# Retention with left-over keys: keys copied by VectorE, values rounded two steps earlier, values stored in rows of 4 KB

## The chip, the cores and the metric

The kernel runs on one core of a Trainium2 chip, in one launch. The metric is device time in microseconds, the median of several runs. TensorE (PE) multiplies, VectorE (DVE), ScalarE (ACT) and GpSimd (POOL) work on its results, SyncE (SP) and POOL issue nearly all DMAs, each on a queue of its own.

## What is computed

The reference is one block of a language model over 528 tokens, 16 meta tokens and 512 real ones: a gated feed-forward layer, a mixer, a second feed-forward layer and a norm. The change lies in the mixer's retention branch. It has four heads with keys of 256 and values of 512 elements. Cut to what matters:

```python
qm, km, vm = q[:, :, :N_META], k[:, :, :N_META], v[:, :, :N_META]          # N_META = 16
state0 = einsum('bhkd,bhke->bhde', km * zeta_m, vm)
def step(state, qkv):                                                      # chunks of 128 tokens
    inner = (qc @ kc.T * d_in) @ vc
    cross = (qc @ state) * xi
    state = g_chunk * state + (kc * zeta).T @ vc
    return state, inner + cross
y = y * rsqrt(mean(y * y) + EPS)
yr = (silu(rg) * y) @ w_ret_out
```

That is the same as causal scores times a decay, times the values. The kernel computes it in that form: for 512 queries and 528 keys, scores times a decay table, then scores times values.

## The kernel before

**Products.** Matmul operands are split in two float32r parts, a high part (ScalarE rounds, `AF.Copy`) and a low part (VectorE subtracts the high part); each product is three matmuls, high by high, high by low, low by high. `steps_through` runs a list of steps. A step has its weight tile loaded (SP), rounded by ScalarE (`upper`, two steps ahead) and its low part made by VectorE (`lower`, called inside an earlier step). TensorE, VectorE and ScalarE work in the order in which the program is written, through the retention part SP too. POOL's order is found by the scheduler that lays out the program: among what is ready, what was written first goes first.

**Values.** The class `Values` (L1333) makes values, gates and attention values of the real tokens two blocks of 128 at a time and stores them in DRAM (`leave`, L1370). `vrs_d` holds head, token, column. The values of the 16 meta tokens come from `last_tokens` (L1395) and are stored in `vd`.

**Where the tokens lie.** In the scores the 528 keys are the 16 meta tokens first. The four full blocks of 128 keys therefore end 16 tokens short of a block of real tokens, and the last 16 keys that a block of 128 queries can see are left over. They are "the last tokens": `last_of` (L1298) names them among the keys, `corner_keys` (L1839) copies them together, `corners` (L1846) multiplies them with the last 16 queries of each block, and one further matmul in `weigh` (L1875) adds their part of the output: its operands are `ptail` (the left-over scores: 32 rows high, 32 low, 32 high again, for two blocks at a time) and `vtail` (the left-over values: high, high again, low). `place_last` (L1624) loads the left-over values to three places of `vtail` by six DMAs on POOL's queue; `split_last` (L1631) rounds two of the three on ScalarE and returns the subtract that makes the third on VectorE.

**One head.** `fetch_head` (L1747) loads values and gates on SP's queue, the values by four DMAs: 112 rows, the meta tokens, and three more blocks. `values_in` (L1767) splits them. `decayed` (L1820) makes four blocks of scores (`psst`, 512 to 128 columns), multiplies each with the decay table (L1828, VectorE, into a buffer `tmp`), and splits it: ScalarE rounds a block, and VectorE makes its low part behind the next block's product. `weigh` (L1864) multiplies scores and values for one block of queries; ScalarE squares and sums the result, VectorE multiplies it with the gate.

**Order in time.** Head 0 is special. The gate steps `start_0` and `start_1` (L2079, L2090) load it, split its values and, in `after_1` (L2083), run `decayed(0)`, the low half of the values, the Silu of its gates and `index_keys(0)` on POOL. The next step, the first query projection of head 1, has 24 matmuls in eight groups of three, 0 to 7; ahead of groups 2 and 5 (L2116) stand `corner_keys` and `corners(0)`, and behind it `weigh_all(0)` (L2094). For heads 1 to 3 the four steps of `outputs(h)` (L1999), each two groups `j` of 12 matmuls, carry the next head: step 0 fetches it, step 1 ends with `values_in`, step 2 with `decayed`, step 3 begins with `corner_keys`, has `corners` behind its first group (after `lower` and `beside`, which does a step of the top-k search on VectorE) and ends with `weigh_all`. From head 1 on, POOL adds each group's output to `accr` (L2025) and makes the low parts of the values (L1774).

**Buffers.** `tmp()` gives one of four buffers of one tag; a buffer is free again when the last reader of its tile is done. `ka` and `kb_`, the index keys and their swapped copy, take two of the four before `decayed(0)` (loads at L1698 and L1700); `index_keys(0)` (L1729 to L1731, on POOL) is the last to read `kb_`, `index_keys(2)` the last to read `ka`. Blocks of scores and other results of up to 512 columns share four PSUM banks (`sm_tile`).

```python
            for kb in range(4):                                   # decayed, L1823
                t = tmp()[:, :n]
                TT(t, ps, u[0][:, :n], ALU.mult)
                low()                                             # low part of the block before
                low = in_two(t, ph, pl)                           # ScalarE now, VectorE later
```

## Time and profile before

| | us |
|---|---|
| median of 3 runs (1478.28 to 1480.94) | 1480.2 |
| the profiled execution's own time | 1479.45 |
| its span, first to last instruction | 1477.5 |
| PE busy | 1460.5 |
| DVE busy | 1153.3 |
| ACT busy | 785.8 |
| POOL busy | 292.4 |

The profile is one execution, taken by the hardware. The span is a little shorter than the execution's own time. A line such as L1875 is a line of the kernel; "out<-in" names the tiles that an instruction writes and reads, and a number in brackets is the time its engine stood idle before it, with what ended that. Of TensorE two rows exist, PE for matmuls and PEld for weight loads; matmuls overlap in the pipeline, so one of 512 columns shows about 0.39 us and the next begins earlier. PEclk is the clock granted to TensorE as a share of 2.4 GHz: 1.00, or 0.50 for 1.2 GHz. Times in timelines count from the start of the span. The mean granted clock of this execution is 0.996.

### The profile page before, as it was taken

The page shows a single profiled execution, that of the slowest core. Times are in us where ns is not written, and L with a number is a line of the kernel's source. Part 1 is how long each engine was busy: PE and PEld are TensorE (multiplying, and loading weights), DVE is VectorE, ACT ScalarE, POOL GpSimd, SP SyncE. Part 2 cuts the span into 40 slices and gives each one's busy share as a digit, 9 for nine tenths or more (in the row PEclk, how much of TensorE's full clock was granted, in tenths as well). Part 3 has the DMA queues.
Part 4 walks back from the last instruction along what each step waited for, and adds up shares of the span by engine and source line. Part 5 has one row for each costly group of instructions (what it writes and reads, how often), then busy time and mean ns, then how long its engine had stood idle before and what let it go on. Part 6 is the DMA issues. An engine that isn't in the chain of part 4 may idle for free.

```text
span 1477.5 us, 22534 instructions
## 1 busy us (share of the span) xinstructions
PE 1460.5 (99%) x8626; PEld 1288.5 (87%) x8626; DVE 1153.3 (78%) x1694; ACT 785.8 (53%) x1137; POOL 292.4 (20%) x363
## 2 busy tenths in 40 slices
PE   9999999999999999999999999999999999999998
PEld 8999999999988888788878788888888888888887
DVE  5998888876887887578778798888657787767776
ACT  6656455455354554467454547777534644434444
POOL 1101111102100001331152442444102221201110
PEclk9999999999999999999999999999999999999999
DMA  5458887556644543564437343767756576466323
GB/s 173 102 157 202 190 186 188 138 127 222 218 149 160 172 161 132 177 196 165 125 122 224 111 150 101 216 176 200 222 183 210 164 219 200 142 199 202 126 79 122
DMA packets 211516, 247.75 MB, mean 168 GB/s; under 512 B 32176, under 2 KB 154024, under 8 KB 211408
## 3 DMA queue, kind: packets, MB, share of 16 engines
q1 hardware_dynamic: 173168, 179.77, 38.4%
q0 software_dynamic: 34320, 59.70, 16.5%
q10 hardware_dynamic: 3920, 6.84, 1.4%
q8 instruction: 68, 1.11, 0.3%
q14 instruction: 40, 0.33, 0.1%
HBM read 206.73 MB, written 39.34 MB: 167 GB/s over the span
## 4 chain that ended last, share of the span: by engine, by line
PE 92%; DVE 3%; ACT 2%; DMA 2%; issue 1%; ACTq 0%; DVEq 0%; SPq 0%
PE psd L2851 8%; PE psqX L2684 7%; PE psvX L1444 7%; PE psqX L162 7%; PE psqZ L162 5%; PE psd L162 4%; PE psqY L2684 4%; PE psvY L1444 4%; PE psak L162 3%; PE psrk L162 3%; PE psaq L162 3%; PE psga L162 3%; PE psat L162 3%; PE psmo L162 3%; PE psrq L162 3%; PE psdX L162 2%
## 5 line engine op out<-in xcount | busy, mean ns | idle before, releaser
L330 DVE TENSOR_TENSOR wlo<-raw,whi 128x1024 fp32r<-128x1024 f32 (+2 forms) x138 | 155.4, 1128 | 35.0 <-ACT whi L329 34.1
L329 ACT ACTIVATE whi<-raw 128x1024 fp32r<-128x1024 f32 (+2 forms) x138 | 130.0, 943 | 85.5 <-PE psat L162 9.4
L330 DVE TENSOR_TENSOR wlo<-w,whi 128x1024 fp32r<-128x1024 f32 x96 | 117.0, 1220 | 62.0 <-ACT whi L329 61.9
L329 ACT ACTIVATE whi<-w 128x1024 fp32r<-128x1024 f32 x96 | 101.6, 1058 | 103.2 <-PE psd L2851 39.6
L162 PE MATMUL psro<-o,whi 128*128 128x512 f32 x256 | 80.3, 395 | 0.0
L329 ACT ACTIVATE whi<-wsum 128x1024 fp32r<-128x1024 f32 (+1 forms) x48 | 48.4, 1008 | 37.1 <-issue 11.8
L119 ACT ACTIVATE whi<-raw 128x1024 fp32r<-128x1024 f32 (+1 forms) x43 | 43.7, 1016 | 35.7 <-PE psat L162 12.2
L120 DVE TENSOR_TENSOR wlo<-raw,whi 128x1024 fp32r<-128x1024 f32 (+1 forms) x43 | 52.8, 1230 | 9.3 <-ACT whi L119 9.2
L2647 POOL DMA_DIRECT2D hts<-cross x40 | 26.0, 657 | 164.9 <-DVE cross L2644 164.9
L2851 PE MATMUL psd<-wlo,hh 128*128 128x512 f32 (+1 forms) x148 | 56.7, 383 | 0.0
L2851 PE MATMUL psd<-whi,hl 128*128 128x512 f32 (+1 forms) x148 | 56.7, 383 | 0.0
L2851 PE MATMUL psd<-whi,hh 128*128 128x512 f32 (+1 forms) x148 | 56.7, 383 | 0.0
L162 PEld LDWEIGHTS psro<-o,whi 128*128 128x128 f32 x256 | 48.0, 190 | 9.7
L330 DVE TENSOR_TENSOR wlo<-wsum,whi 128x1024 fp32r<-128x1024 f32 (+1 forms) x48 | 55.3, 1154 | 1.4 <-ACT whi L329 0.9
L162 PE MATMUL psro<-o,wlo 128*128 128x512 f32 x128 | 50.6, 395 | 0.0
L2025 POOL TENSOR_TENSOR accr<-accr,RR 128x512 f32<-128x512 f32 x24 | 37.0, 1546 | 63.2 <-ACT RR L2024 60.6
L1444 PE MATMUL psvX<-wlo,th 128*128 128x512 f32 x120 | 46.8, 390 | 0.0
L1444 PE MATMUL psvX<-whi,tl 128*128 128x512 f32 x120 | 46.7, 389 | 0.0
L1444 PE MATMUL psvX<-whi,th 128*128 128x512 f32 x120 | 46.7, 389 | 0.0
L162 PE MATMUL psqX<-xh,wlo 128*128 128x264 f32 x144 | 40.8, 283 | 0.0
L162 PE MATMUL psqZ<-xh,wlo 128*128 128x264 f32 x144 | 40.8, 283 | 0.0
L162 PE MATMUL psqX<-th,wlo 128*128 128x264 f32 x144 | 40.7, 283 | 0.0
(634 smaller groups left out, 5040.4 us busy)
## 6 DMA issues: line engine op xcount, KB each, us to landing
w<-in_w_in_dram SPq DMA_DIRECT2D x40, 512.0 KB, 4.6
raw<-in_w_in_dram SPq DMA_DIRECT2D x27, 512.0 KB, 4.1
raw<-in_w_in_dram SPq DMA_DIRECT2D x13, 1024.0 KB, 6.6
raw<-in_ffn_w_down_dram SPq DMA_DIRECT2D x24, 512.0 KB, 4.4
raw<-in_ffn_w_up_dram SPq DMA_DIRECT2D x11, 1024.0 KB, 5.1
raw<-in_ffn_w_gate_dram SPq DMA_DIRECT2D x10, 1024.0 KB, 5.3
ws<-in_ffn_w_up_dram POOLq DMA_DIRECT2D x20, 512.0 KB, 6.0
w<-in_ffn_w_up_dram SPq DMA_DIRECT2D x20, 512.0 KB, 5.0
```

The lines of the kernel that those rows point to most:

```text
L119: nc.scalar.activation(hi, src, AF.Copy)
L120: eng.tensor_tensor(lo, src, hi.bitcast(F32), ALU.subtract)
L162: nc.tensor.matmul(o, a[:, k, :], b[:, sl], start=first and k == 0 and i == 0, stop=last and k == nk - 1 and i == 2, skip_group_check=onto)
L329: nc.scalar.activation(hi, src, AF.Copy)
L330: return lambda: nc.vector.tensor_tensor(lo, src, hi.bitcast(F32), ALU.subtract)
L1444: nc.tensor.matmul(d[bank_][t], a, b[:, k, :], start=not onto and j + k + m == 0, stop=j + k == 3 and m == 2, skip_group_check=onto)
L2025: nc.gpsimd.tensor_tensor(a, a, t, ALU.add)
L2647: nc.gpsimd.dma_start(d.rearrange("(b i) a e -> a i b e", i=32)[a], cross[32 * a : 32 * a + 32].rearrange("p b c t -> p b (c t)"))
L2684: nc.tensor.matmul(ps[:, t], a, b[:, k, :], start=not onto and j + k + m == 0, stop=j + k == 3 and m == 2, skip_group_check=onto)
L2851: nc.tensor.matmul(ps, a, m[:, j, cs], start=first and i == 0, stop=last and i == 2)
```

## The change

The values move 16 tokens on in DRAM, so that the meta tokens stand in front: `vrs_d` becomes head, partition, block, column, with the meta tokens in block 0, and one partition's rows of all blocks lie side by side. `leave` stores each pair of blocks by two DMAs (112 partitions and 16 partitions, 4 KB each), `last_tokens` stores the meta tokens by four DMAs in place of one, `fetch_head` loads the values by two DMAs in place of four, and `place_last` loads the left-over values of head 0 once instead of three times. `split_last(0)` makes the two rounded parts by two ScalarE copies from that one place; it is called ahead of group 1 of the query step, with its subtract at once. For the later heads `split_last` moves from `corners` (step 3) to the end of step 0, and its subtract to the end of step 1 ahead of `values_in`. The left-over keys are copied by VectorE instead of ScalarE, inside `decayed` behind the second block. In `corners` the second copy of the high scores is made by POOL from the first instead of by ScalarE. `corners(0)` comes ahead of group 4 instead of 5, and in step 3 `corners` goes ahead of `beside`. `vd` keeps only the attention's tails, at new places.

```diff
@@ -299,10 +299,10 @@
 
 
     vst = dpool.tile([2, P, 4, 4, P], F32, name="vst")
-    vrs_d = dpool.tile([RH, S, S], F32, name="vrs")
+    vrs_d = dpool.tile([RH, P, 5, S], F32, name="vrs")
     rgs = dpool.tile([RH, 2, P, 2 * S], F32, name="rgs")
     ots = dpool.tile([2, 2, S, 4, 64], F32, name="ots")
-    vd = dpool.tile([6, 2, P, P], F32, name="vd")
+    vd = dpool.tile([2, 2, P, P], F32, name="vd")
     fq = dpool.tile([P, 4, S], F32, name="fq")
     fs = dpool.tile([P, 4, S], F32, name="fs")
     fk = dpool.tile([2, P, T], F32, name="fk")
@@ -1373,8 +1373,8 @@
                     nc.gpsimd.dma_start(vst[i, :, :, 2 * half : 2 * half + 2, :].rearrange("p c b d -> p c (b d)"),
                                         r.rearrange("p (c b d) -> p c (b d)", b=2, c=4))
                 elif self.kind == "values":
-                    nc.gpsimd.dma_start(vrs_d[i, half * 2 * P : (half + 1) * 2 * P].rearrange("(b p) c -> p b c", p=P),
-                                        r.rearrange("p (b c) -> p b c", b=2))
+                    for rows, to, b in ((slice(0, P - NM), slice(NM, P), 0), (slice(P - NM, P), slice(0, NM), 1)):
+                        nc.gpsimd.dma_start(vrs_d[i, to, 2 * half + b : 2 * half + b + 2].rearrange("p b c -> p (b c)"), r[rows])
                 else:
                     nc.gpsimd.dma_start(rgs[i, half], r)
 
@@ -1405,12 +1405,13 @@
                 r = room("rest")[:, : 4 * P]
                 if self.kind == "values":
                     nc.scalar.activation(r[:, : 2 * P], ps[:, : 2 * P], AF.Copy)
-                    nc.gpsimd.dma_start(vd[2 * self.u : 2 * self.u + 2, 0].rearrange("i p d -> p i d"),
-                                        r[:, : 2 * P].rearrange("p (i d) -> p i d", i=2))
+                    for c in range(4):
+                        nc.gpsimd.dma_start(vrs_d[2 * self.u : 2 * self.u + 2, :NM, 0, c * P : (c + 1) * P].rearrange("i q d -> q i d"),
+                                            r[32 * c : 32 * c + NM, : 2 * P].rearrange("q (i d) -> q i d", i=2))
                     return
                 split(ps[:, : 2 * P], r[:, : 2 * P].bitcast(F32R), r[:, 2 * P :].bitcast(F32R))
                 for i in range(2):
-                    nc.gpsimd.dma_start(vd[2 * self.u + i + 4 * (self.kind == "heads")].rearrange("i p d -> p i d"),
+                    nc.gpsimd.dma_start(vd[i].rearrange("i p d -> p i d"),
                                         r.rearrange("p (i s d) -> p i s d", i=2, s=2)[:, :, i, :])
 
             def take(self, bank_, r):
@@ -1623,15 +1624,18 @@
 
     def place_last(h):
 
-        rows = vrs_d[h].rearrange("(a b p) c -> b p a c", a=2, p=P)
-        for r in (4, 0, 2):
+        for r in (4, 0, 2) if h else (4,):
             for b in range(2):
-                nc.gpsimd.dma_start(tp["v"][(r + b) * NM : (r + b + 1) * NM].bitcast(F32), rows[b, P - NM :])
-
-    def split_last():
+                nc.gpsimd.dma_start(tp["v"][(r + b) * NM : (r + b + 1) * NM].bitcast(F32), vrs_d[h, :NM, 1 + b :: 2])
+
+    def split_last(h):
 
         t, n = tp["v"], 2 * NM
-        nc.scalar.activation(t[: 2 * n], t[: 2 * n].bitcast(F32), AF.Copy)
+        if h:
+            nc.scalar.activation(t[: 2 * n], t[: 2 * n].bitcast(F32), AF.Copy)
+        else:
+            for i in range(2):
+                nc.scalar.activation(t[i * n : (i + 1) * n], t[2 * n : 3 * n].bitcast(F32), AF.Copy)
         return lambda: nc.vector.tensor_tensor(t[2 * n : 3 * n], t[2 * n : 3 * n].bitcast(F32), t[:n].bitcast(F32), ALU.subtract)
 
     def values_of(parts):
@@ -1751,12 +1755,8 @@
             else:
                 v = vraw().rearrange("p (b c) -> p b c", b=4)
                 vparts["l"] = [v[:, :2], v[:, 2:]]
-            a, b = vparts["l"]
-            rows = vrs_d[h, P - NM : S - NM].rearrange("(b p) c -> b p c", p=P)
-            nc.sync.dma_start(a[NM:, 0], vrs_d[h, : P - NM])
-            nc.sync.dma_start(a[:NM, 0].rearrange("q (c d) -> q c d", c=4), vd[h, 0].rearrange("(c q) d -> q c d", q=32)[:NM])
-            nc.sync.dma_start(a[:, 1], rows[0])
-            nc.sync.dma_start(b, rows[1:].rearrange("b p c -> p b c"))
+            for i, v in enumerate(vparts["l"]):
+                nc.sync.dma_start(v, vrs_d[h, :, 2 * i : 2 * i + 2])
             heads[h]["g"] = [room4("g") for _ in range(2)]
             for half in range(2):
                 nc.sync.dma_start(heads[h]["g"][half], rgs[h, half].rearrange("p (b c) -> p b c", b=2))
@@ -1817,6 +1817,15 @@
                 for i, (a, b) in enumerate(((0, 0), (0, 1), (1, 0))):
                     nc.tensor.matmul(ps, keys[k][a], queries(ret_q[k][b]), start=k == 0 and i == 0, stop=k == 1 and i == 2)
 
+        corner = {}
+
+        def corner_keys():
+
+            last_k = tmp().bitcast(F32R)[:, : 4 * NT].rearrange("p (a b q) -> p a b q", a=4, q=NM)
+            for do, of in zip((last_k[:, :, :3], last_k[:, :, 3]), last_of):
+                nc.vector.tensor_copy(do, of.bitcast(F32))
+            corner["k"] = last_k
+
         def decayed(h):
             rk, u = ret_k, heads[h]["u"]
             prob, low = [], lambda: None
@@ -1831,22 +1840,14 @@
                 pl = rt.tile([P, n], F32R, tag=f"pl{kb}", name="pl")
                 low = in_two(t, ph, pl)
                 prob.append((ph, pl))
+                if kb == 1:
+                    corner_keys()
             low()
             heads[h]["prob"] = prob
 
-        corner = {}
-
-        def corner_keys():
-
-            last_k = tmp().bitcast(F32R)[:, : 4 * NT].rearrange("p (a b q) -> p a b q", a=4, q=NM)
-            for do, of in zip((last_k[:, :, :3], last_k[:, :, 3]), last_of):
-                nc.scalar.activation(do, of.bitcast(F32), AF.Copy)
-            corner["k"] = last_k
-
         def corners(h):
 
             last_k, u = corner["k"], heads[h]["u"]
-            low = split_last()
             ps = sm_tile("psst")[:NT, :NT]
             scored(ps.rearrange("p (b q) -> p b q", q=NM), [[last_k[:, 2 * j + i].rearrange("p b q -> p (b q)") for j in range(2)] for i in range(2)], lambda t: t.rearrange("p (b q) -> p b q", q=P)[:, :, P - NM :])
             t = tmp()[:NT, :NT]
@@ -1857,9 +1858,8 @@
                 src = t[at, at].rearrange("p (b q) -> p b q", q=NM)
                 h_, l_, again = (last[i * 2 * NM : (i + 1) * 2 * NM, a, :, P - NM :] for i in range(3))
                 nc.scalar.activation(h_, src, AF.Copy)
-                nc.scalar.activation(again, src, AF.Copy)
                 TT(l_, src, h_.bitcast(F32), ALU.subtract)
-            low()
+                nc.gpsimd.tensor_copy(again, h_.bitcast(F32))
 
         def weigh(h, b):
 
@@ -2005,8 +2005,6 @@
                         ap = mx["acc"] = accs.enter_context(pool("acc", 1, side="right"))
                         acc_r.extend(ap.tile([P, S], F32, tag=f"accr{c}", name=f"accr{c}") for c in range(KD))
                         vr["pool"] = vrs.enter_context(pool("vraw", 1, side="right"))
-                    if i == 3 and h + 1 < RH:
-                        corner_keys()
                     if i == 0 and h + 1 < RH:
                         fetch_head(h + 1)
                         new_decay(h + 1)
@@ -2025,11 +2023,14 @@
                             nc.gpsimd.tensor_tensor(a, a, t, ALU.add)
                         if j == 0:
                             lower()
-                            beside(i)
                             if i == 3 and h + 1 < RH:
                                 corners(h + 1)
+                            beside(i)
                     if h + 1 < RH:
+                        if i == 0:
+                            heads[h + 1]["last"] = split_last(h + 1)
                         if i == 1:
+                            heads[h + 1]["last"]()
                             values_in(h + 1)
                         if i == 2:
                             decayed(h + 1)
@@ -2113,7 +2114,7 @@
         gr = tiles("gr", w_in, OFF_GR, 7)
         more = steps_of(gr[:2], [start_0, start_1])
         nothing = lambda: None
-        more += queries_keys(1, (beside_q0, beside_q1, lambda: fetch_turned(0, 1), nothing), (((2, corner_keys), (5, lambda: corners(0))), (), ((3, lambda: (index_queries(4), index_keys(2))), (5, first_pairs)), ((6, pair),)))
+        more += queries_keys(1, (beside_q0, beside_q1, lambda: fetch_turned(0, 1), nothing), (((1, lambda: split_last(0)()), (4, lambda: corners(0))), (), ((3, lambda: (index_queries(4), index_keys(2))), (5, first_pairs)), ((6, pair),)))
         come = [(i, lambda half=half: arrived(0, (half,))) for half, i in enumerate((1, 5))]
         more += steps_of(gr[2:4], [proj("psgate", REAL, (*come, *((i, pair) for i in (2, 4, 6, 7))), later_gate(2)),
                                    proj("psgate", REAL, tuple((i, pair) for i in (1, 3, 5, 6, 7)), after_3)])
@@ -2370,7 +2371,7 @@
                     t = gate_a(tile or mm_tile("psga")[:, :S], between)
                     nc.gpsimd.dma_start(gd[KD + ga.at - 1], t)
 
-            place_tails(4)
+            place_tails(0)
             with tc.manual_schedule(engines=BUSY):
                 w = cq.next()
                 yk = Swapped(first_k, cos, sin, 64, T)
@@ -2471,7 +2472,7 @@
                     transpose_block(2, ends[2])
                     transpose_tail()
                 if h == 4:
-                    place_tails(5)
+                    place_tails(1)
                 if 0 < h < 7:
                     t = at.tile([P, S], F32, tag="gate", name="gate", bufs=2)
                     nc.scalar.dma_start(t, gd[h - 1])
```

## Rows read from the trace of the kernel before

**Rows 1.** The page: busy time, share of the span and instructions of each engine.

```profile
PE 1460.5 (99%) x8626; PEld 1288.5 (87%) x8626; DVE 1153.3 (78%) x1694; ACT 785.8 (53%) x1137; POOL 292.4 (20%) x363
```

**Rows 2.** Waits of TensorE: line, releaser, us in total, times, longest.

```profile
PE psst L1818 <- ACT tmp L1843: 6.5, 4, 1.8
PE psst L1818 <- ACT RR L1968: 1.5, 1, 1.5
...
PE pspv L1875 <- ACT accr L2021: 0.6, 1, 0.6
...
PE pspv L1875 <- ACT RR L2024: 0.4, 1, 0.4
```

**Rows 3.** Windows: length, busy PE, PEld, DVE, ACT, POOL, PEclk, DMA.

```profile
765.98:769.39 3.41, 3.41 (x10) 2.64 (x9) 2.28 (x5) 1.08 (x5) 0.34 (x1) 0.50 0.01 2
```

**Rows 4.** Timeline of TensorE in head 0: start, us, engine, line.

```profile
624.25 0.88 PE L1818 MATMUL psst<-rqk 128*128 128x128 f32 x6 [1.49 <-ACT RR L1968]
624.97 0.45 PE L162 MATMUL psrq<-xh,whi 128*128 128x512 f32 x1
...
631.89 0.54 PE L1818 MATMUL psst<-rqk,tmp 128*64 128x64 f32 x6 [1.69 <-ACT tmp L1843]
...
636.69 0.40 PE L1875 MATMUL pspv<-vtail,ptail 96*128 96x512 f32 x1
```

**Rows 5.** Timeline of ScalarE in head 0.

```profile
622.66 1.06 ACT L1771 ACTIVATE vh<-vl 128x1024 fp32r<-128x1024 f32 x1 [3.17 <-DMA vl<-vrs]
...
630.40 1.04 ACT L329 ACTIVATE whi<-raw 128x1024 fp32r<-128x1024 f32 x1
631.35 0.49 ACT L1843 ACTIVATE tmp<-rqk 128x192 fp32r<-128x192 f32 x2
631.75 1.04 ACT L1634 ACTIVATE vtail<-vtail 64x1024 fp32r<-64x1024 f32 x1
```

**Rows 6.** Timeline of TensorE in head 2.

```profile
761.78 0.62 PE L162 MATMUL psro<-o,whi 128*128 128x512 f32 x2
762.24 0.39 PE L162 MATMUL psro<-o,wlo 128*128 128x512 f32 x1
764.35 0.54 PE L1818 MATMUL psst<-rqk,tmp 128*64 128x64 f32 x6 [1.73 <-ACT tmp L1843]
```

**Rows 7.** Groups of POOL's instructions: count, busy us, mean ns, idle before.

```profile
L1629 POOL DMA_DIRECT2D vtail<-vrs x24 | 12.4, 530 | 8.1 <-PE pspv L1875 8.1
...
L1376 POOL DMA_DIRECT2D vrs<-part x8 | 5.7, 714 | 56.1 <-DVE part L1418 40.3 <-ACT part L1466 9.2 <-DVE part L1456 6.5
...
L1594 POOL COPY bias<-caus 128x128 f32<-128x128 f32 x1 | 0.3, 289 | 1.9 <-DMA caus<-in_causal_dram 1.9
```

**Rows 8.** Waits of SP's queue.

```profile
SPq L138 <- DVE wlo L330: 274.2, 42, 46.4
```

**Rows 9.** Timeline of TensorE in head 1.

```profile
709.88 0.47 PE L1875 MATMUL pspv<-vtail,ptail 96*128 96x512 f32 x1 [0.60 <-ACT accr L2021]
```

**Rows 10.** Timeline of VectorE in head 1.

```profile
708.56 1.22 DVE L1635 TENSOR_TENSOR vtail<-vtail 32x1024 fp32r<-32x1024 f32 x1
```

**Rows 11.** Timeline of VectorE in head 2.

```profile
755.97 2.02 DVE L330 TENSOR_TENSOR wlo<-raw,whi 128x1024 fp32r<-128x1024 f32 x1 [1.22 <-ACT whi L329]
...
759.35 1.49 DVE L330 TENSOR_TENSOR pl<-tmp,ph 128x512 fp32r<-128x512 f32 x1 [0.27 <-ACT ph L329]
...
763.95 1.21 DVE L330 TENSOR_TENSOR wlo<-raw,whi 128x1024 fp32r<-128x1024 f32 x1
```

**Rows 12.** Timeline of POOL in heads 0 and 2.

```profile
635.09 2.28 POOL L1731 TENSOR_TENSOR tmp<-tmp 64x512 f32<-64x512 f32 x1
...
760.25 3.29 POOL L2025 TENSOR_TENSOR accr<-accr,RR 128x512 f32<-128x512 f32 x2
```

**Rows 13.** Timeline of VectorE in head 0.

```profile
624.75 0.69 DVE L330 TENSOR_TENSOR pl<-tmp,ph 128x512 fp32r<-128x512 f32 x1 [2.10 <-DMA tmp<-fs]
625.55 0.42 DVE L1828 TENSOR_TENSOR tmp<-psst,RR 128x256 f32<-128x256 f32 x1
```

## The prediction

> **What bounds the kernel now.** I read the page first. TensorE is busy for 1460.5 of 1477.5 us [rows 1], so a change here can win what TensorE loses to waits and to the low clock, and no more. Next, TensorE's waits [rows 2]: 6.5 us in four pieces are matmuls of the corner scores (L1818) waiting for ScalarE's copy of the left-over keys (L1843); 1.5 us is the fourth score block of head 0 waiting for the gate's sigmoid (L1968); 0.6 and 0.4 us are the left-over matmul of the outputs (L1875). Third, the windows: after head 2's stall a stretch of 3.41 us ran at half the granted clock, 1.2 instead of 2.4 GHz [rows 3]. Head 0 shows two more such stretches, from 626.0 and from 632.9, each behind a stall of TensorE; each costs half its length, 1.7 us.
>
> Then the timelines of head 0. TensorE starts the fourth score block at 624.25, the first query matmul at 624.97, the corner scores at 631.89 and the first left-over matmul at 636.69 [rows 4]. On ScalarE the second half of the values waited 3.17 us for its load, which held up the sigmoid; later two Silu and a weight rounding stand ahead of the key copies, and the 1.04 us rounding of the left-over values behind them [rows 5]. In head 2 two matmuls start 0.46 us ahead of a third, so 0.23 us each; the corner scores begin 2.11 us after that third, 1.88 later than they could, against 1.73 shown as idle [rows 6]: the views leave out about 0.15 us for each wait.
>
> **The change, part by part.** The sum is made against the profiled execution: 1479.45 us, its span of 1477.5 and 1.95 around it; the median of 1480.2 lies 0.75 above.
>
> *Rows of 4 KB.* Storing the values takes 16 DMAs on POOL's queue instead of 8, and the left-over tokens 8 instead of 2: 14 more at 0.71 us, 10 us of POOL. Ahead of the stores POOL stands idle for 56 us [rows 7], so I cost them at nothing. Without that cover the stores would land later, not the matmuls: the values are read only after three more units of products. Fetching takes 8 DMAs on SP's queue instead of 16, and place_last 20 on POOL's instead of 24, at 0.53 us each [rows 7]. SP spends its time waiting for free weight buffers [rows 8], so issues saved there are worth nothing. The move of vd's index changes no operation. What can count is when head 0's second half lands: four loads of 64 KB (16 partitions of two rows of 2 KB) go from beside it. Lower bound: no earlier, and the fourth block starts at 624.25 as now. Upper bound: TensorE is ready 1.49 us earlier, at 622.76. I take 623.2, nearer the second, since those four loads are a quarter of a megabyte out of the stretch in which ScalarE waited.
>
> *Heads 1 to 3.* VectorE copies the keys between the second and third block of decayed, so the corner scores no longer wait for ScalarE. Gone: 6.5 less head 0's 1.69, 4.8; the L1875 waits, 1.0. The views name ScalarE's copies as their releasers, but in head 1 the matmul at 709.88 follows VectorE's subtract of the left-over values (L1635, 1.22 us), which ends at 709.78 [rows 9, 10]; that subtract is now at the end of step 1. Further gone: 0.15 for each of these five, 0.7; head 2's half clock, 1.7. Together -8.2. split_last's 1.04 us on ScalarE moves to the end of step 0, where it waits for DMAs issued tens of microseconds before.
>
> What is late next: in heads 2 and 3 VectorE. Its subtract now stands ahead of a weight subtract that has 1.22 us of idle before it, but lies in a stretch where such a subtract takes 2.02 us instead of 1.21 [rows 11]; two key copies (0.49 us on ScalarE [rows 5], which I use for VectorE too) follow, beside POOL's adds. Then come the weight subtract (1.21 us), the corner product, ScalarE's rounding, a subtract, and the second copy, now POOL's, at 0.29 each at most [rows 7], behind an add of 1.65 us (two take 3.29 [rows 12]). If VectorE is 1.25 us later than now, the weight subtract starts at 765.2 and the tail matmul can go at 767.2; TensorE gets there at 762.47 + 0.54 (the six corner matmuls) + 15 x 0.23 = 766.5. So about 0.7, with bounds 0 (idle time swallows all) and 1.5 (both contended at their longest). I take 0.9 for each head, above the middle because the copies are contended too: +1.8. Head 1 has no adds on POOL, and I take 0. Putting corners ahead of beside moves the top-k pick behind it, which helps and delays nothing TensorE waits for.
>
> The contention is a row first: the 128x512 subtract takes 0.69 us in head 0 and 1.49 where POOL's adds begin in head 2 [rows 11 to 13]. The Trainium skill (SBUF — State Buffer, Who interferes with whom) states it harder: the port pair of VectorE and GpSimd is an exclusive lock, held for a whole instruction by a VectorE copy in its two-port mode against any GpSimd operation. By that rule a key copy could wait out a whole add, 1.65 us, in each of the two heads, and the sum would come to about 1477.6; the rows agree in kind and show half of that, 0.8.
>
> *Head 0.* Here a wait is added. The pool of products has four buffers: the index keys and their swapped copy hold two until POOL's index_keys, and decayed alternates between the others. Now the copied keys take the third, freed by the first product, before the third product is made; the second's buffer is freed only by an instruction behind the third product on VectorE. So the third product must wait, either for the corner scores to have read the keys or for POOL's L1731. The corner scores come first in every order that I can derive: they stand after 12 query matmuls and wait for neither. From 623.2, 0.72 for the fourth block [rows 4], 12 x 0.23 and 0.54 give 627.2, against 625.55 now [rows 13].
>
> Behind that product on VectorE are its own low part, the fourth product and the low half of the values; on ScalarE two roundings, two Silu, a weight rounding and then two split_last copies (1.04 each [rows 5]) instead of one; and TensorE waits for all of them. In the trace of before the weight rounding is done at 631.44, 5.9 us after the third product starts; two copies make it 7.9 (consecutive ones start 1.0 apart); the 1.22 us subtract [rows 10] 9.1; the corner product, two roundings and low parts at 0.2 each and POOL's copy of 0.29 make it 10.3. The tail matmul goes at 637.5 instead of 636.69, +0.8, and TensorE, there at 627.2 + 15 x 0.23 = 630.6, idles for 7 us; half clock behind it adds about 1.5. Head 0: +2.3. Bounds: start at 622.76 gives 637.0, +1.8 in all; start at 624.25 puts the third product at 628.3, or at 629.7 with seven of the twelve matmuls at half clock as now, and the tail at 640.0, +4.8 in all.
>
> Sum: -8.2 + 1.8 + 2.3 = -4.1, or 1475.4 by the profiled execution and 1476.1 by the median: 1476.
>
> **The rivals.**
> A, *slower*: the third product gets the buffer that POOL's L1731 frees. That ends at 637.37 [rows 12], since POOL waits for its tables. Then the tail goes at 637.4 + 10.3 = 647.7, +11.0, with 1.7 of half clock: -8.2 + 1.8 + 12.7 = +6.3, 1486.5. It decides as soon as L1731 is the releaser. For it: POOL frees one of the four. Against: a dozen DMA issues and waits for three tables stand ahead of it on POOL. 10%.
> B, *nothing to see*: both bounds at their bad end, head 0 at +4.8 and heads 2 and 3 at 1.5 each: -0.4, 1480; or POOL's copies in head 0 stand behind L1594 and L1731, with about the same end. For it: the load was slowed by much more than vtail. Against: two bad ends are needed. 20%.
> C, *more*: nothing holds the third product in head 0. Then it starts at 624.8 behind the copies and the tail goes at 635.1, still held by Silu and split_last; with half clock head 0 comes to 0, and the sum to -6.4 or a little more: 1473. 14%.
>
> **How the numbers follow.** The forecast, 1476 (1473.5 to 1478.5), has 56%. 1471.5 to 1481.5 takes in C, most of B and the forecast's bounds; A and the outer ends are left out. A measurement of this kernel tells 0.2%, 3 us, from no change, so faster means below 1477.2: three quarters of the forecast, C, and a little of B, 0.58. Slower than 1483.2 is A and little else, 0.11. The rest is 0.31.
>
> **What would show it.** Right: no wait of L1818 for key copies in heads 1 to 3, no half clock behind head 2; in head 0 one idle of 6 to 8 us ahead of L1875, and VectorE idle ahead of the third L1828, released by TensorE's corner scores. Waits of L1875 in heads 2 and 3 under 1.5 us, released by POOL or VectorE. Wrong: that product released by POOL (A), or not waiting (C); an idle in head 0 under 4 us; the fourth block starting at 624.2 or later; or new waits before 600 or after 840 us, where I expect none.

## The result and the profile after

The changed kernel takes 1493.39 us in the median of six runs (1489.32 to 1494.62) against 1480.74 for the kernel before beside it: a ratio of 1.0083, with a 95% interval from 1.0068 to 1.0098. It is slower; the forecast of 1476 and its range to 1481.5 were wrong. The profiled execution has a span of 1491.2 us, 13.7 more than before.

On the page TensorE is busy 3.2 us longer than in [rows 1], VectorE 10.7 us with only eight more instructions, POOL 4.5 us longer, ScalarE 1.7 us shorter. What was added to the span is mostly idle time of TensorE, with some time at the low clock; VectorE's longer time is the first sign that its instructions wait.

```profile
PE 1463.7 (98%) x8626; PEld 1291.2 (87%) x8626; DVE 1164.0 (78%) x1702; ACT 784.1 (53%) x1122; POOL 296.9 (20%) x381
```

TensorE's waits answer to [rows 2]; the columns are the same.

```profile
PE psst L1818 <- DVE tmp L1837: 11.0, 3, 4.5
PE pspv L1875 <- POOL ptail L1862: 6.7, 1, 6.7
...
PE psst L1818 <- ACT RR L2022: 0.2, 1, 0.2
```

The waits for key copies and for the sigmoid are gone, as forecast. In their place stand three long waits in the scores of heads 1 to 3, for VectorE's product (L1837, which was L1828), and one in head 0, for the left-over tile.

Two of the four stretches at half clock in the four heads, as windows (columns as in [rows 3]); the other two are 3.41 us long, in heads 1 and 3:

```profile
636.38:643.21 6.83, 5.25 (x12) 4.13 (x13) 3.75 (x8) 1.95 (x6) 0.39 (x2) 0.50 0.17 59
769.50:776.33 6.83, 5.73 (x17) 4.77 (x18) 5.90 (x12) 2.72 (x5) 2.81 (x2) 0.50 0.00 1
```

Head 2 shows how heads 1 to 3 lose. First TensorE's timeline, against [rows 6]:

```profile
762.34 2.58 PE L1818 MATMUL psst<-rqk 128*128 128x512 f32 x12
765.16 0.97 PE L1818 MATMUL psst<-rqk 128*128 128x256 f32 x6 [0.24 <-ACT RR L2022]
770.60 1.54 PE L1818 MATMUL psst<-rqk 128*128 128x128 f32 x6 [4.46 <-DVE tmp L1837]
```

VectorE's timeline there, against [rows 10, 11]:

```profile
763.46 3.19 DVE L1639 TENSOR_TENSOR vtail<-vtail 32x1024 fp32r<-32x1024 f32 x1
766.85 3.09 DVE L330 TENSOR_TENSOR wlo<-raw,whi 128x1024 fp32r<-128x1024 f32 x1 [0.20 <-DVE vtail L1639]
769.86 1.14 DVE L1837 TENSOR_TENSOR tmp<-psst,RR 128x512 f32<-128x512 f32 x2
```

And POOL's, where [rows 12] showed only the additions:

```profile
763.15 5.70 POOL L1774 TENSOR_TENSOR vraw<-vraw,vh 128x1024 fp32r<-128x1024 f32 x2
768.82 3.49 POOL L2023 TENSOR_TENSOR accr<-accr,RR 128x512 f32<-128x512 f32 x2
```

In the kernel before, POOL's two value subtracts stood there too, around the weight subtract of 2.02 us [rows 11]:

```profile
754.47 5.82 POOL L1774 TENSOR_TENSOR vraw<-vraw,vh 128x1024 fp32r<-128x1024 f32 x2
```

The fourth block of scores waits for a place in PSUM that the first product must have read. That product stands behind the moved subtract of the left-over values (L1639, 1.22 us in [rows 10], here 3.19) and behind a weight subtract (2.02 in [rows 11], here 3.09). Both lie beside POOL's two value subtracts, 5.70 us together. TensorE has finished the first two blocks by 764.92; their products start at 769.86.

Head 0 went nearly as forecast. TensorE, VectorE and ScalarE there, one fence each, against [rows 4, 13, 5]:

```profile
630.39 0.39 PE L1874 MATMUL pspv<-vh,ph 128*128 128x512 f32 x1
...
637.96 0.80 PE L1875 MATMUL pspv<-vtail,ptail 96*128 96x512 f32 x1 [6.71 <-POOL ptail L1862]
```

```profile
627.77 0.43 DVE L1837 TENSOR_TENSOR tmp<-psst,RR 128x256 f32<-128x256 f32 x1 [2.88 <-PE psst L1818]
...
635.76 1.22 DVE L1639 TENSOR_TENSOR vtail<-vtail 32x1024 fp32r<-32x1024 f32 x1 [4.32 <-ACT vtail L1638]
637.01 0.22 DVE L1854 TENSOR_TENSOR tmp<-psst,ulast 64x64 f32<-64x64 f32 x1
```

```profile
630.65 2.00 ACT L1784 ACTIVATE g<-g 128x1024 f32<-128x1024 f32 x2
632.56 1.04 ACT L329 ACTIVATE whi<-raw 128x1024 fp32r<-128x1024 f32 x1
633.61 2.12 ACT L1638 ACTIVATE vtail<-vtail 32x1024 fp32r<-32x1024 f32 x2
```

The third product is held until the corner scores have read the copied keys (2.88 us of idle ahead of it, released by TensorE), and the gates, a weight and two roundings follow on ScalarE. TensorE idles for 6.7 us, and its next 5.25 us, to 643.21, run at half clock.

### The profile page after: what moved, and what is told of

Read it like the earlier page. It is cut to its first block, busy times and chain, and to the rows that moved or that the text cites. A ratio compares the mean times of both kernels' runs of the same rounds, so it can differ in the third digit from the quotient of the medians.

```text
span 1491.2 us, 22544 instructions
## 1 busy us (share of the span) xinstructions
PE 1463.7 (98%) x8626; PEld 1291.2 (87%) x8626; DVE 1164.0 (78%) x1702; ACT 784.1 (53%) x1122; POOL 296.9 (20%) x381
## 4 chain that ended last, share of the span: by engine, by line
PE 92%; DVE 3%; DMA 2%; ACT 1%; issue 1%; ACTq 0%; DVEq 0%; SPq 0%; POOL 0%; POOLq 0%
PE psd L2852 8%; PE psvX L1445 7%; PE psqX L2685 7%; PE psqX L162 7%; PE psqZ L162 5%; PE psd L162 4%; PE psqY L2685 4%; PE psvY L1445 4%; PE psro L162 3%; PE psak L162 3%; PE psrk L162 3%; PE psaq L162 3%; PE psga L162 3%; PE psat L162 3%; PE psmo L162 3%; PE psgate L162 3%
## 5 line engine op out<-in xcount | busy, mean ns | idle before, releaser
L330 DVE TENSOR_TENSOR wlo<-raw,whi 128x1024 fp32r<-128x1024 f32 (+2 forms) x138 | 159.3, 1156 | 36.3 <-ACT whi L329 35.2
L162 PE MATMUL psro<-o,whi 128*128 128x512 f32 x256 | 83.3, 408 | 0.0
L162 PE MATMUL psqX<-th,whi 128*128 128x264 f32 x144 | 40.8, 283 | 0.0
```

Source lines behind the costliest of these rows:

```text
L162: nc.tensor.matmul(o, a[:, k, :], b[:, sl], start=first and k == 0 and i == 0, stop=last and k == nk - 1 and i == 2, skip_group_check=onto)
L330: return lambda: nc.vector.tensor_tensor(lo, src, hi.bitcast(F32), ALU.subtract)
```

## The experiments

The profiles before and after the retention stage scatter by one to three us from run to run, whatever the edit, so I read each head by itself: a **stretch** is the time from the head's first score matmul (psst) to the end of its last output matmul (pspv). After, head 2's goes from 762.34 to 788.00, 25.66 us. Between the stretches lie 53.3, 38.6 and 38.6 us in every kernel, to within 0.05. The four stretches grew by 2.6 + 2.6 + 4.4 + 2.6 = 12.2 us of the 13.7. Each stretch comes from one profiled execution, and in best2, no_sub, keys0 and head0_old that was the fastest of the kernel's runs.

| kernel | median us | ratio to before [95%] | head 0 | head 1 | head 2 | head 3 |
|---|---|---|---|---|---|---|
| before | 1480.74 | | 24.45 | 20.08 | 21.29 | 20.37 |
| the change | 1493.39 | 1.0083 [1.0068, 1.0098] | 27.07 | 22.67 | 25.66 | 23.01 |
| sub_at_end | 1486.64 | 1.0034 [1.0022, 1.0046] | 27.41 | 19.67 | 22.03 | 22.16 |
| sub_step0 | 1483.32 | 1.0012 [1.0000, 1.0024] | 27.37 | 18.67 | 21.83 | 21.46 |
| only_sub | 1491.71 | 1.0062 [1.0046, 1.0079] | 24.20 | 22.67 | 23.25 | 25.84 |
| lows_dve | 1490.25 | 1.0055 [1.0042, 1.0068] | 27.23 | 21.26 | 25.46 | 22.94 |
| keys0 | 1492.56 | 1.0067 [1.0049, 1.0084] | 27.38 | 22.70 | 23.03 | 22.85 |
| split0 | 1491.09 | 1.0057 [1.0040, 1.0073] | 25.79 | 24.04 | 23.03 | 22.94 |
| head0 | 1489.72 | 1.0056 [1.0040, 1.0073] | 25.23 | 24.02 | 23.10 | 23.15 |
| head0_old | 1488.77 | 1.0048 [1.0035, 1.0061] | 22.24 | 22.65 | 24.84 | 23.06 |
| best | 1482.56 | 1.0014 [1.0002, 1.0025] | 26.04 | 18.67 | 23.16 | 21.52 |
| layout | 1479.08 | 0.9987 [0.9978, 0.9996] | 22.26 | 20.08 | 20.99 | 20.12 |
| keys_act | 1482.07 | 0.9993 [0.9979, 1.0007] | 27.17 | 18.41 | 21.51 | 20.05 |
| again_act | 1483.86 | 1.0011 [1.0000, 1.0022] | 26.84 | 18.59 | 22.94 | 21.32 |
| best2 | 1477.06 | 0.9963 [0.9950, 0.9977] | 20.84 | 18.30 | 20.19 | 19.81 |
| no_sub | 1474.82 | 0.9957 [0.9940, 0.9974] | 22.26 | 17.91 | 18.99 | 18.41 |
| sub_after_scores | 1479.81 | 0.9981 [0.9966, 0.9995] | 22.23 | 18.59 | 23.53 | 21.79 |

The same head of the same code can differ by 1.4 to 2.6 us from profile to profile, where a stretch at half clock is there or not, or is longer. Head 2 of the change is the largest case: 25.66 us, but 23.03 to 24.84 in keys0, split0, head0 and head0_old, which have heads 1 to 3 in the change's order too. The kernel before had medians from 1480.7 to 1483.0 beside the groups of runs, so kernels of different groups are compared by their ratios.

**The moved subtract.** Theory: it waits for POOL's value subtracts. Rivals: VectorE's key copies hold the products, or head 0 is most of the loss. Put back behind the corners:

```diff
                 nc.gpsimd.tensor_copy(again, h_.bitcast(F32))
+            if h:
+                heads[h]["last"]()
...
                         if i == 1:
-                            heads[h + 1]["last"]()
```

> The change, with the subtract of the left-over values in heads 1 to 3 put back behind the corners; all else stays. Theory (the moved subtract waits for POOL's two value subtracts, and the weight subtract behind it waits too): VectorE's vtail subtract is back at about 1.2 us, the weight subtract behind the scores at 1.2 to 2.1 us instead of 3.1, the waits for the first product of the scores (11.0 us in three) fall to under 6, and the time to 1479 to 1485 us against 1493.4 for the change. Rival 1 (the copies of the left-over keys on VectorE, with their buffer, hold the products) and rival 2 (head 0's tail, 3.9 us later by my account, is most of the loss): 1491 to 1495 us, waits for the products unchanged.

Or one step earlier:

```diff
                         if i == 0:
                             heads[h + 1]["last"] = split_last(h + 1)
-                        if i == 1:
                             heads[h + 1]["last"]()
+                        if i == 1:
```

> The change, with that subtract one place earlier: right behind ScalarE's rounding at the end of the outputs' first step, where POOL has no value subtract (in heads 2 and 3 an addition of 1.3 us). Theory: the subtract takes 1.2 to 2.5 us there and delays a weight subtract that is not yet wanted; nothing is left at the corners; waits of the products under 5 us in all, time 1475 to 1482 us, and at or under the run with the subtract at the end. If instead any move of the subtract ahead of the scores costs the same (VectorE's order and not POOL's subtract): 1488 to 1494 us. Rivals 1 and 2: 1491 to 1495.

Or alone, in the kernel before:

```diff
-            low = split_last()
+            low = heads[h]["last"] if h else split_last()
...
-            low()
+            if not h:
+                low()
...
+                        if i == 0:
+                            heads[h + 1]["last"] = split_last()
                         if i == 1:
+                            heads[h + 1]["last"]()
                             values_in(h + 1)
```

> The kernel before, with one thing of the change: in heads 1 to 3 ScalarE rounds the left-over values at the end of the first step and VectorE subtracts at the end of the second. Theory: the vtail subtract takes 2.8 to 3.5 us and the weight subtract behind it about 3.1, as in the change, and the time goes from 1480.7 to 1487 to 1494 us. Rivals 1 and 2: within 2 us of the kernel before.

All three go with the theory. only_sub slows the kernel before by 9.8 us in the medians; its subtract takes 2.85, 3.20 and 3.45 us in heads 1 to 3, and three waits of 11.2 us in all are there. It has head 0 and the key copies as before, so neither rival can be its cause. Put back at the end, the subtract takes 1.22 us; the waits for products come to 0.9 us, but the tail product now waits for it, 6.0 us in three. That run came out 1.6 us above the range that I wrote. At the first step it takes 1.22 to 1.49, the three stretches are 61.96 us together against 71.34, and no half clock is left in heads 1 to 3. That run is 1.3 us above its range. The ratio falls from 1.0083 to 1.0012. With another head 0 the same move takes it from 1.0056 to 1.0014 (head0 to best, below): the place of one subtract a head costs 0.4 to 0.7%.

Is it POOL, or one instruction too many on VectorE? With POOL's value subtracts on VectorE as well:

```diff
-                eng = nc.gpsimd if h else nc.vector
+                eng = nc.vector
```

> The change, with the value subtracts of heads 1 to 3 (two a head of 2.85 us each on POOL) on VectorE too. VectorE gets two instructions of about 1.22 us a head more, POOL has none beside them. If the subtracts wait for each other: the vtail subtract and the weight subtract behind it take 1.2 us each instead of 2.8 to 3.5 and 3.1, the first product of the scores comes about 1.5 us earlier although two more instructions stand ahead of it, the stretches of heads 1 to 3 (22.67, 25.66, 23.01 us) get 1.5 to 3 us shorter each, and the time is 1485 to 1489.5 us against 1493.4. If VectorE simply has one instruction too many ahead of the scores: the products come 2.4 us later and the time is 1496 to 1502 us.

In head 1 POOL has nothing else to do, and the row answers. VectorE after, then POOL after, then VectorE of lows_dve, all in head 1:

```profile
700.58 2.84 DVE L1639 TENSOR_TENSOR vtail<-vtail 32x1024 fp32r<-32x1024 f32 x1
703.62 3.15 DVE L330 TENSOR_TENSOR wlo<-raw,whi 128x1024 fp32r<-128x1024 f32 x1 [0.20 <-DVE vtail L1639]
706.69 1.14 DVE L1837 TENSOR_TENSOR tmp<-psst,RR 128x512 f32<-128x512 f32 x2
```

```profile
699.92 5.76 POOL L1774 TENSOR_TENSOR vraw<-vraw,vh 128x1024 fp32r<-128x1024 f32 x2 [13.50 <-ACT vh L1771]
```

```profile
701.01 1.22 DVE L1639 TENSOR_TENSOR vtail<-vtail 32x1024 fp32r<-32x1024 f32 x1
702.32 2.36 DVE L1774 TENSOR_TENSOR vraw<-vraw,vh 128x1024 fp32r<-128x1024 f32 x2
704.59 1.22 DVE L330 TENSOR_TENSOR wlo<-raw,whi 128x1024 fp32r<-128x1024 f32 x1
705.73 1.15 DVE L1837 TENSOR_TENSOR tmp<-psst,RR 128x512 f32<-128x512 f32 x2
```

POOL's two of the changed kernel one by one, then VectorE of sub_step0 in head 1:

```profile
699.92 2.41 POOL L1774 TENSOR_TENSOR vraw<-vraw,vh 128x1024 fp32r<-128x1024 f32 x1 [13.50 <-ACT vh L1771]
702.31 3.37 POOL L1774 TENSOR_TENSOR vraw<-vraw,vh 128x1024 fp32r<-128x1024 f32 x1
```

```profile
692.56 1.22 DVE L1639 TENSOR_TENSOR vtail<-vtail 32x1024 fp32r<-32x1024 f32 x1
...
701.03 1.66 DVE L330 TENSOR_TENSOR wlo<-raw,whi 128x1024 fp32r<-128x1024 f32 x1 [1.23 <-ACT whi L329]
```

After the change the two engines take turns. POOL's first subtract ends at 702.33 and VectorE's of the left-over values at 703.42, 1.09 us later; POOL's second ends at 705.68 and VectorE's of the weight at 706.77, again 1.09 us later. Each VectorE subtract thus waits for POOL's to end and then takes about its own time (1.22). With the moved subtract away, the weight subtract has the first turn: in sub_step0 it ends 2.8 us after the head's first score matmul (699.92), after the change 5.7 us (701.06).

From the start of the moved subtract to the first product it is 6.11 us after the change, with two subtracts beside POOL's, and 4.72 in lows_dve, with four and no partner. VectorE did twice the work in three quarters of the time. The stretch got 1.4 us shorter; heads 2 and 3 stayed within 0.2, for there POOL's additions take the value subtracts' place (the two on VectorE take 3.44 us in head 2, the weight subtract 2.28). So the time was 1490.25, above the range that I had written for the theory, though far from the rival's.

**Head 0.** Its stretch grew by 2.6, but against the layout alone, below, by 4.8. First the key copies back in the projection:

```diff
-                if kb == 1:
+                if kb == 1 and h:
                     corner_keys()
...
-(((1, lambda: split_last(0)()), (4, lambda: corners(0))), ...
+(((1, lambda: split_last(0)()), (2, corner_keys), (4, lambda: corners(0))), ...
```

> The change, with head 0's copies of the left-over keys put back into the projection (still on VectorE), so that the third block's product finds its buffer free. By my account the product then runs at about 624.9 us instead of 627.8, ScalarE is through with the table load and the gates 2.5 to 3 us earlier, and the first tail product comes at about 635 instead of 638: 1489.5 to 1491.5 us against 1493.4. Rival 2 (head 0 is most of the loss): 1486 or less. If ScalarE's next weights come no earlier: no change, 1493.

A miss that teaches. The third product is free, ScalarE is through early (gates at 626.3), and the tail's wait is gone, but the copies now stand behind the late subtract on VectorE, and the corner scores wait instead. VectorE, then TensorE, of keys0:

```profile
631.43 1.22 DVE L1639 TENSOR_TENSOR vtail<-vtail 32x1024 fp32r<-32x1024 f32 x1 [4.96 <-ACT vtail L1638]
632.69 0.36 DVE L1826 CAST tmp<-rqk 128x192 fp32r<-128x192 f32 x2
```

```profile
633.10 0.85 PE L1818 MATMUL psst<-rqk,tmp 128*64 128x64 f32 x6 [6.88 <-DVE tmp L1826]
```

6.7 us at the tail became 6.9 at the corner scores. Next the roundings ahead of the blocks, alone and with the keys moved:

```diff
             later_gate(1)(ps)
+            split_last(0)()
             decayed(0)
...
-(((1, lambda: split_last(0)()), (4, lambda: corners(0))), ...
+(((4, lambda: corners(0)),), ...
```

> The change, with head 0's two roundings on ScalarE and the subtract on VectorE put ahead of the four blocks of scores (the rows have landed at about 621.9 us) instead of behind the gates and a weight rounding. If head 0's lateness is ScalarE's order: the roundings run at about 622 to 624, the first tail product follows the weight rounding (633.6) at about 634.5 instead of 638.0, and the stretch at half clock behind it gets shorter: 1487.5 to 1490.5 us against 1493.4. If the held buffer alone makes it late: no more than 1 us.

```diff
-(((1, lambda: split_last(0)()), (4, lambda: corners(0))), ...
+(((2, corner_keys), (4, lambda: corners(0))), ...
```

(with the two lines of split0 in after_1 and that of keys0 in decayed)

> Both parts of head 0 at once: the roundings and the subtract ahead of the blocks, and the key copies in the projection, now with no late subtract ahead of them on VectorE; heads 1 to 3 as in the change. The last run but this left them behind that subtract, and the corner scores waited 6.9 us for them. Expected: third block's product not held (about 2.9 us), corner scores and first tail product with under 2 us of wait together, no half clock for 6.8 us behind it: 1483 to 1487 us. If PE has another wait to take at that place (the corner chain itself, two small operations on ScalarE behind the weight rounding): 1487 to 1490.

Both give back less than I wrote, 1.3 and 1.8 us of the stretch. The subtract stands ahead of the products on VectorE and waits for two roundings, and TensorE waits 1.6 and 1.7 us for a product at the queries instead; with split0 3.0 us of wait at the tail are left, with head0 2.3 for the key copies. Last, the whole head as before:

```diff
-        for r in (4, 0, 2) if h else (4,):
+        for r in (4, 0, 2):
...
-        if h:
-            nc.scalar.activation(t[: 2 * n], ...)
-        else:
-            for i in range(2):
-                ...
+        nc.scalar.activation(t[: 2 * n], t[: 2 * n].bitcast(F32), AF.Copy)
...
-(((1, lambda: split_last(0)()), (4, lambda: corners(0))), ...
+(((2, lambda: corner_keys(lambda o, i: nc.scalar.activation(o, i, AF.Copy))), (5, lambda: corners(0))), ...
```

(in corners, head 0 alone takes the split and its subtract, and the second copy on ScalarE)

> The change, with head 0 wholly in the order of before: three copies of its left-over values by DMA, one rounding of 64 rows, the split and the subtract at the corners, key copies and both rounded corner copies on ScalarE; heads 1 to 3 as in the change. If head 0's loss comes from these steps together: its stretch goes from 27.1 to 20.8 to 22.5 us and the time from 1493.4 to 1487 to 1489.5 us. If it comes from elsewhere (the layout's DMAs, what stands ahead): above 25 us and 1492 or more.

22.24 us, the layout's own value: head 0's loss is its own order, 4.8 us, part of it the longer stretch at half clock (6.83 us in the change, 3.41 here). Neither of the two steps taken back alone gave it back (keys0 nothing, split0 1.3), nor both (1.8); the other steps were not taken back one by one.

**Both mended**, sub_step0 and head0 in one kernel:

```diff
                         if i == 0:
                             heads[h + 1]["last"] = split_last(h + 1)
-                        if i == 1:
                             heads[h + 1]["last"]()
+                        if i == 1:
...
             later_gate(1)(ps)
+            split_last(0)()
             decayed(0)
```

(with the two lines on the key copies of head0)

> The change, with both of its faults mended: the subtract of heads 1 to 3 at the end of the first step (1483.3 us by itself) and head 0 as in the run before. If the two losses lie at different places and add up: 1473.5 to 1478 us, under the kernel before (1480.7). If they do not (one hides the other): 1479 to 1484.

1482.56 was not under the kernel before: head 0 still has 26.04 us, and heads 2 and 3 are not better than before. So what else of the change costs?

**The other parts.** The layout alone, in the kernel before (the change's lines for the storing, the source in place_last, fetch_head and vd, and no others):

```diff
-    vrs_d = dpool.tile([RH, S, S], F32, name="vrs")
+    vrs_d = dpool.tile([RH, P, 5, S], F32, name="vrs")
...
-            nc.sync.dma_start(a[NM:, 0], vrs_d[h, : P - NM])
...
+            for i, v in enumerate(vparts["l"]):
+                nc.sync.dma_start(v, vrs_d[h, :, 2 * i : 2 * i + 2])
```

> The kernel before, with the change's storing of the values alone (16 partitions on, rows of 4 KB, two loads a head instead of four; the tails' columns in the same array); the left-over values still come as three copies, all orders as before. In head 0 the second half of the values lands earlier, so the fourth block's wait (1.5 us) goes: 1478 to 1480.7 us by my theory. Rival (the layout or its smaller DMAs costs something that I laid on the subtract): 1483 or more.

A gain of 0.13%: head 0 is 2.2 us shorter. Its four blocks run as one group without the wait of 1.49 us in [rows 4]; the wait ahead of the corner scores is 1.1 us longer, and one of the two stretches at half clock is gone:

```profile
620.08 3.90 PE L1818 MATMUL psst<-rqk 128*128 128x512 f32 x24
630.29 0.54 PE L1818 MATMUL psst<-rqk,tmp 128*64 128x64 f32 x6 [2.82 <-ACT tmp L1826]
```

Then, in sub_step0, the key copies of heads 1 to 3 on ScalarE at the same place:

```diff
+            copy = nc.vector.tensor_copy if h == 0 else lambda o, i: nc.scalar.activation(o, i, AF.Copy)
             for do, of in zip((last_k[:, :, :3], last_k[:, :, 3]), last_of):
-                nc.vector.tensor_copy(do, of.bitcast(F32))
+                copy(do, of.bitcast(F32))
```

> The kernel with the subtract at the first step (1483.3 us), and the left-over key copies of heads 1 to 3 at the same place of the scores but on ScalarE; head 0 unchanged. In that kernel the two copies took 2.52 us on VectorE in head 2 beside two of POOL's additions (763.5 to 766.5 us) and 0.35 where no addition ran, and the corner scores waited 1.0 us for them in heads 2 and 3. If the copies wait for POOL's additions: on ScalarE they take about 0.5, the waits for them go, and heads 2 and 3 (21.83 and 21.46 us from the first product of the scores to the last tail product) get 0.8 to 1.5 us shorter each, head 1 (18.67) stays: 1480.3 to 1482 us. If another VectorE instruction only takes the copies' place beside the additions and the products are as late as before: the stretches stay within 0.4 us, 1483.

VectorE in head 2 of sub_step0, then POOL there:

```profile
761.23 1.14 DVE L1837 TENSOR_TENSOR tmp<-psst,RR 128x512 f32<-128x512 f32 x2
762.66 1.45 DVE L330 TENSOR_TENSOR pl<-tmp,ph 128x512 fp32r<-128x512 f32 x1 [0.29 <-ACT ph L329]
764.03 2.52 DVE L1826 CAST tmp<-rqk 128x192 fp32r<-128x192 f32 x2
```

```profile
757.79 5.77 POOL L1774 TENSOR_TENSOR vraw<-vraw,vh 128x1024 fp32r<-128x1024 f32 x2
763.52 2.98 POOL L2023 TENSOR_TENSOR accr<-accr,RR 128x512 f32<-128x512 f32 x2
```

The two copies, 0.35 us where POOL is idle, end with POOL's second addition. On ScalarE the wait for them is gone, and the three stretches come to 59.97 against 61.96. The size was right in head 3 (1.4); head 2 has a new wait of 1.4 us for ScalarE's copy of the outputs, which again_act shows there too, and gained 0.3.

The second copy of the rounded corners on ScalarE, again in sub_step0:

```diff
-                nc.gpsimd.tensor_copy(again, h_.bitcast(F32))
+                if h:
+                    nc.scalar.activation(again, src, AF.Copy)
+                else:
+                    nc.gpsimd.tensor_copy(again, h_.bitcast(F32))
```

> The same kernel with the second copy of the rounded corners of heads 1 to 3 on ScalarE again, as before the change, head 0 unchanged. On POOL it stood behind an addition of 1.8 us in head 2 (769.4 to 771.3) and the tail product waited 0.9 us in heads 2 and 3. Expected if that is the cause: waits under 0.4 us, heads 2 and 3 each 0.4 to 0.7 shorter (two more ScalarE instructions of 0.23 us stand in the chain), head 1 within 0.3: 1481.8 to 1482.8 us. If the low parts on VectorE beside the addition set it: no change, 1483.3.

No gain: the ratio stays (1.0011), and 0.7 us of wait are left in heads 2 and 3, now named after ScalarE. My reading of that wait fell: POOL's copy alone does not set it.

**A version from what is left:** the layout kernel with the key copies at the same place in the scores but on ScalarE, the split of heads 1 to 3 with its subtract at the first step, the corners ahead of beside:

```diff
+                if kb == 1 and h:
+                    corner_keys()
...
-            low = split_last(1)
+            low = split_last(1) if h == 0 else lambda: None
...
+                        if i == 0:
+                            split_last(1)()
```

(and the lines that take corner_keys out of the fourth step and put the corners ahead of beside)

> What the runs leave of the change: the new layout (1479.1 us by itself), the split of the left-over values of heads 1 to 3 at the end of the first step, the corners ahead of the selection in the fourth; but key copies in the scores on ScalarE, the second rounded copy on ScalarE, and head 0 in the order of before with its three copies of the values. Expected by the stretches: head 0 22.3, head 1 18.7 to 19.2, heads 2 and 3 20 to 20.6 us against 22.3, 20.1, 21.0 and 20.1 in the run of the layout alone: 1476 to 1478.5 us, below both kernels. If ScalarE's order in the scores (a copy of 0.5 us ahead of a block's rounding) gives it back: 1479 to 1481.

It is faster than before by 0.37%, the best of all kernels that compute the whole, and its profile has no half clock in the four heads. 1.4 us of head 0's gain, at 20.84, is that alone: four other kernels with head 0 in this order have 22.2 to 22.3 and one stretch of 3.41 us at half clock. Last, what the subtract costs even there, left out or put behind the scores:

```diff
-                            split_last(1)()
+                            split_last(1)
```

> The kernel best2 with the subtract of heads 1 to 3 left out (their left-over values have a rounded part and no low part, so that part of the output is less exact). If the subtract at the end of the first step still costs by delaying VectorE's rotation and the products: the fourth block's wait (1.2 us in heads 2 and 3) falls under 0.4 and heads 2 and 3 (20.19 and 19.81 us) come to 18.8 to 19.3, as head 1 (18.30) stays: 1475 to 1476 us against 1477.1. If what remains is ScalarE's or POOL's part (value roundings and additions ahead of the products): unchanged within 0.4 us a head, 1476.5 to 1477.5.

```diff
-                            split_last(1)()
+                            heads[h + 1]["last"] = split_last(1)
...
                             decayed(h + 1)
+                            heads[h + 1]["last"]()
```

> The kernel best2 with that subtract behind the scores, at the end of the third step, where VectorE has 0.6 us of idle ahead of a weight subtract and POOL nothing to do. Expected if the subtract costs by its place at the first step: products 1.2 us earlier, the weight subtract and the corner product 0.6 later, heads 2 and 3 each 0 to 1 us shorter, head 1 up to 0.5 longer: 1475.5 to 1477.5 us. If it delays the corners by its whole length: 1478 to 1480.

Left out, it takes 3.0 us off the three stretches (58.30 to 55.31), 2.6 of it in heads 2 and 3, and the fourth block's waits fall from 2.5 us to 0.5. The times do not separate the two kernels: 0.9957 against 0.9963, with overlapping intervals. Behind the scores it is worse. VectorE of sub_after_scores in head 2:

```profile
765.26 1.22 DVE L1639 TENSOR_TENSOR vtail<-vtail 32x1024 fp32r<-32x1024 f32 x1
766.59 2.12 DVE L330 TENSOR_TENSOR wlo<-raw,whi 128x1024 fp32r<-128x1024 f32 x1
768.63 0.21 DVE L1855 TENSOR_TENSOR tmp<-psst,ulast 64x64 f32<-64x64 f32 x1
```

The subtract itself is not slowed. The weight subtract behind it is (2.12 us; 1.21 at 762.26 in best2's head 2), the tail product waits 4.7 us in three, and half clock is back in heads 2 and 3.

## Why the prediction was wrong

- **The step that failed** is "What is late next", sized at +1.8 with bounds 0 and 1.5 a head, and within it "Head 1 has no adds on POOL, and I take 0". I looked for POOL's additions beside the subtract and overlooked POOL's value subtracts, which stand at the end of the same step in all three heads. The row was there: the 2.02 us that I quoted for a weight subtract [rows 11] is that instruction beside L1774, and I took the stretch for merely slower. I added 1.25 us for one subtract; it and the one behind it took 6.0 to 6.6 us, because each waits for one of POOL's to end. The term measured, over heads 1 to 3: 9.4 us for its place by the change and sub_step0 (71.34 against 61.96) and 6.9 by head0 and best (70.27 against 63.35), and 3.0 for the subtract at the first step (best2 to no_sub, in their profiles alone).
- **The rule that I cited was read too narrowly.** I quoted it for the key copies alone. The Trainium skill (SBUF — State Buffer, Who interferes with whom) says too that a VectorE instruction with two SBUF inputs contends with a GpSimd instruction that reads SBUF. The Trainium skill (SBUF — State Buffer, Summary: rules for kernel authors) says that the second of the two to issue is blocked until the first finishes. The trace agrees: 2.84, 3.19 and 3.46 us for 1.22, each ending about 1.1 us behind POOL's first subtract. In sub_step0 the product L1837, which has one input in PSUM, keeps 1.14 us for two beside L1774. My "half of that" for the copies was too little where they meet POOL: 2.52 us for two in sub_step0. In the changed kernel they came behind the additions and took 0.35.
- **The gain of heads 1 to 3**, -8.2: the waits named did go. With the subtract left out and the copies on ScalarE the three stretches fall from 61.74 to 55.31, 6.4 us. By that kernel the term was 1.8 too large. Against it stand, in the profiles, the 9.4 and 3.0 above and 3.7 from sub_step0 (61.96) to best2 (58.30). Those two differ in the key copies, which are 2.0 by keys_act, and in the second corner copy, which gained nothing by itself; 1.7 stays unexplained. That these differences add up to the 9.6 of the table (71.34 - 61.74) proves nothing, since each starts from the kernel at which another ends. With heads 1 to 3 in the change's order, five profiles have 68.6 to 71.3 us, so each size is uncertain by one to two us.
- **Head 0**, +2.3: its stretch grew by 2.6. The third product was held by the corner scores, as I said, and started at 627.8 (forecast 627.2); the tail came at 638.0 (637.5), behind 6.7 us of idle (7). In this profile all of head 0 starts 1.2 us later, so the tail itself is not late against before; the 2.6 us are the low clock behind it, which I had at 1.5. So the hold was right and the total agrees partly by luck: 0.8 too much for the tail, 1.1 too little for the clock. The layout's part in it was right in kind and larger than I had it: 2.2 us alone, and the orders cost 4.8.
- **The rivals.** A did not occur: TensorE's corner scores released the third product. B and C did not either. The slower outcome had 11%, put on head 0's buffer; the place where it came from had no rival of its own.
- **What I said would show it**: the key waits gone, the one idle in head 0, no long L1875 waits in heads 2 and 3, all so. No half clock behind head 2: wrong, 6.83 us of it. New waits before 600 us, one of the signs of being wrong: one of 1.1 us stands at 185.8 us, but it comes and goes whatever the edit (only_sub and head0 have it, keys0 and sub_step0 do not). That the score blocks themselves could come to wait for VectorE's products stood nowhere among the signs.

Open: why head 2 shows a wait of 1.4 us for the outputs' copy in some kernels and not in others, and which of head 0's steps costs how much; only their sum is settled.

## What to carry to other kernels

Before an instruction is moved on VectorE, list what POOL runs in the stretch it goes to, every group and not only the one already in mind; here a subtract of two SBUF tiles waited there until POOL's instruction had ended, and pushed the next one beside POOL's next. A row that is slower than its like elsewhere (2.02 against 1.21) has a partner, to be named before a term is built on it. And a wait removed at one place is worth only what the next instruction in the same engine's order leaves of it: keys0 turned 6.7 us at the tail into 6.9 at the corner scores.

## What the runs showed of the hardware

A subtract over 32 partitions waits like one over 128: 2.84 to 3.46 us beside POOL's subtracts, 1.22 alone. POOL waits too: its first value subtract takes 2.41 us in head 1, its second 3.37. In every profile in which POOL makes them, a VectorE subtract of two SBUF tiles is still running for 1.1 us when the second begins, the moved one after the change and the weight's in the kernel before and in sub_step0; no run shows the second by itself. So POOL's two together took as long with the moved subtract (5.70 us in head 2) as without (5.77 in sub_step0). And the same wait of 2.8 us for the key copies in head 0 has a stretch of 3.41 us at a granted clock of 0.50 around it in the layout kernel and none in best2: what a wait of that size costs in clock differs from run to run. The waits of 4.5 and 6.7 us after the change had 6.83 us each; in head 1 a wait of 3.08 us had 3.41 us after the change and 6.83 in split0.
